# Output stage of a three-stage fp32 trunk: two inner products brought forward by a block, and another order of buffer slots

## Chip, cores, metric

The kernel runs on one core of one Trainium2 chip. The metric is the device time of one execution in microseconds. The engines are called by what they do here: TensorE (PE; PEld is its weight load), VectorE (DVE), ScalarE (ACT), GpSimd (POOL), and SP, which only issues transfers.

## The reference

One layer (DEPTH = 1), 4096 tokens of width 1024, all in float32:

```
normed = rms_norm(x, norm_w)
u, gate = split(normed @ pool_in_w)                  # 1024 -> 2 x 1024
pooled  = trailing_mean(u, window 2/4/8/16 by group) - u
mixed   = pooled @ group_w (4 groups of 256) + group_b
y       = mixed * pool_scale * silu(gate)
out     = rms_norm(x + y @ pool_out_w, final_norm_w)
```

## The kernel before

**Stages.** The group map is folded into the input weights at the start. The steps in the list `steps` follow: kind "a" and kind "b" make the two halves of the channels of y for four blocks of 1024 tokens each; kind "o" is the output stage, y @ out_w with residual and final norm, for eight blocks of 512 tokens (blocks 0 to 7). The change lies in the output stage alone.

**A block of the output stage.** The matrix product of a block is done in the Strassen-Winograd way: each operand is cut into four quarters (11, 12, 21, 22), and seven products P1 to P7 of sums of quarters replace eight. They run in the order P1, P7, P6, P2, P5, P4, P3 (ORDER_OUT); each is one step. Of y, "11" and "12" make the rows of half 0, "21" and "22" those of half 1. All partial results stay in PSUM: of the eight banks a block uses four pairs, "x" (P1, P2), "v" (P7, P4), "y" (P6, P5, P3) and "spare", which rotate by three pairs from block to block. P1 is copied from x to y, so that later products add to it.

**Precision.** An operand is split into a high part (a ScalarE copy to fp32r) and a low part (a VectorE subtraction); a product is high x high, high x low and low x high. `split` issues both, `high` and `low` one each. `mm3` (L805) issues the three matmuls of a plain product, 128x512; a plain product of the output stage is 24 of them (two row quarters j, four k, three parts).

**Inner products.** P2 and P7 of a block may themselves be done by seven smaller products, the leaves: `leaf` (L947), six matmuls of 128x256 each, 42 for a product. Their weights are sums of quarters of P2's or P7's weights: `load_inner` loads the raw ones, `sum_inner` makes the sums (four VectorE subtractions or additions), `split_weight` the high and low parts, into places that are kept from the pool for good (`gathered`, six in all). Leaves P6 and P5 of inner P2 are run in the step of the outer P5, by `product_out` and `evict_o`, and `add_inner` (VectorE) adds the leaves' results to the rows. In the kernel before, inner P2 runs from block 2 on and inner P7 (`own_first`, `own_into`, `own_move`, `own_add`) from block 3 on: OWN = 3. The table `forming` says in which step the weights are made.

**The order.** Up to P5 of block OWN - 1 a scheduler places the instructions of each engine, held by hints (`issue_after`). From P4 of block OWN - 1 on, `steady` writes the order by hand, and `InOrder` keeps each of VectorE, ScalarE, GpSimd and SP in that order; P2 of the last block turns that off again.

**Buffers.** Operands, rows and temporaries share two pools of slots, st (11) and vt (8); `take` gives the slot that has been free longest, `give` puts one at the end. So the order of `give` and `take` decides which earlier user a new one must wait for. A block's rows (x, to which the product is added) take four slots: two for half 1 (`load_h(b, 1)`), two for half 0 (`load_h(b, 0)`); each slot holds a row quarter's 1024 columns. In all blocks but the last, ScalarE writes the product into a half of the columns, x is added by an accumulating transfer that GpSimd issues (`add_h`), or loaded by SP first. `norm_row` scales the finished rows and stores them (`out<-...`, issued by GpSimd): half 1 of block b - 1 in P1's step of block b, half 0 in P6's step. In `steady`, `load_y` fetches the next block's quarters of y from DRAM (yd): 11 and 21 in P7's step, 12 and 22 in P4's step, where 11 is also split for the next P1.

Of the kernel before, what the change touches and what calls it, by code (L numbers as in the profile page):

```python
# [25 lines left out]
HIST = 16  # L26
NS = 11
NV = 8
OWN = 3
EPS = 1e-6  # L30

P1, P2, P3, P4, P5, P6, P7 = range(1, 8)
# [54 lines left out]
def kernel(  # L87
# [57 lines left out]
    st = Slots(sts)  # L145
# [826 lines left out]
    def own_add():  # L972
        bank = own["v"][1].rearrange("p (j b) -> p j b", j=2)
        add(bank, bank, own["m5"].unsqueeze(1).to_broadcast([P, 2, 256]))
# [214 lines left out]

    def split_o(b, i):  # L1190
        s = oxs[b]
        if i == P2 and b > 1:
            return split_inner(s["12"])
        t = next_op("p (s a b) -> p s a b", s=2, a=4)
        if i == P7:
            s["3"] = take("p (a b) -> p a b", a=4)
            sub(s["3"], s["11"], s["21"])
        elif i == P6:
            add(s["21"], s["21"], s["22"])
            sub(s["11"], s["21"], s["11"])  # L1200
        elif i == P3:
            sub(s["12"], s["12"], s["11"])
            give(s.pop("11"))
        key = {P1: "11", P7: "3", P6: "11", P2: "12", P5: "21", P4: "22", P3: "12"}[i]
        split(t, s[key])
        if i not in (P1, P6, P2):
            give(s.pop(key))
        return t
# [293 lines left out]
    def steady(n):  # L1502

        _, b, i = steps[n]
        sets, s, c = sets_of("o", b), oxs[b], b + 1
        final, t = c == NBO, None
        ahead = oxs[c] if not final else None
        whole = dict(a=4, s=2)
        if b < OWN:
            ready[i] = split_up.pop(n)  # L1510
        if i == P1:
            past = sets_of("o", b - 1)
            if final:
                load_h(b, 1)
            t = ready.pop(P1)
            out_part(P1, t, sets["x"][0], 0, range(4))
            square_rows(b - 1, 0, past, 0)
            copy(sets["y"][0], sets["x"][0])
            factor(b - 1, 1)
            add(s["21"], s["21"], s["22"])  # L1520
            sub(s["11"], s["21"], s["11"])
            ready[P6] = next_op("p (s a b) -> p s a b", **whole)
            split(ready[P6], s["11"])
            with tc.issue_after(latest[0]):
                out_part(P1, t, sets["x"][1], 1, range(2))
            own_first(ready.pop(P7), sets)
            with tc.issue_after(latest[0]):
                out_part(P1, t, sets["x"][1], 1, range(2, 4))
            copy(sets["y"][1], sets["x"][1])
            square_rows(b - 1, 0, past, 1)  # L1530
            for j in range(2):
                norm_row(b - 1, 1, j)
        elif i == P7:
            if final:
                load_h(b, 0)
            else:
                ahead["11"] = load_y(c, 0, 0)
                ahead["21"] = load_y(c, 1, 0)
            own_into(P2, 0)
            own_into(P6, 1)  # L1540
            own_move(2, 1)
            a11, a21, a12, a22 = row_quarters(s["12"])
            v = temp(0, "p (n k c) -> p n k c", n=4, k=2)
            sub(v[:, 0], a11, a21)
            sub(v[:, 1], a22, v[:, 0])
            add(v[:, 2], v[:, 1], a11)
            sub(v[:, 3], a12, v[:, 1])
            plain_op, both = op_halves()
            split(both, s["12"])
            root(b - 1, 0)  # L1550
            with tc.issue_after(latest[0]):
                out_part(P6, ready[P6], sets["y"][0], 0, range(2))
            own_into(P7, 2)
            own_into(P3, 1)
            own_move(3, 2)
            with tc.issue_after(latest[0]):
                out_part(P6, ready[P6], sets["y"][0], 0, range(2, 4))
            own_into(P4, 2)
            factor(b - 1, 0)
            ready[P2] = {  # L1560
                p: [plain_op[:, k, g, j] for k in range(2)]
                for p, (g, j) in {P1: (0, 0), P2: (1, 0), P4: (1, 1)}.items()
            }
        elif i == P6:
            v = temp(0, "p (n k c) -> p n k c", n=4, k=2)
            sums_op = next_op("p (s n k c) -> p s n k c", s=2, n=4, k=2)
            high(sums_op, v)
            low(sums_op, v)
            own_add()
            norm_row(b - 1, 0, 0)  # L1570
            norm_row(b - 1, 0, 1)
            for m, p in enumerate((P7, P6, P5, P3)):
                ready[P2][p] = [sums_op[:, k, m] for k in range(2)]
            ready[P5] = next_op("p (s a b) -> p s a b", **whole)
            split(ready[P5], s["21"])
            give(s.pop("21"))
            if not final:
                load_h(b, 1)
            evict_o(b, P7, sets)
            with tc.issue_after(latest[0]):  # L1580
                out_part(P6, ready.pop(P6), sets["y"][1], 1, range(4))
            evict_o(b, P6, sets)
        elif i == P2:
            if not final:
                load_h(b, 0)
            ready[P4] = next_op("p (s a b) -> p s a b", **whole)
            split(ready[P4], s["22"])
            give(s.pop("22"))
            InOrder.on = not final
            product_out(P2, ready.pop(P2), sets, False)  # L1590
            evict_o(b, P2, sets)
        elif i == P5:
            sub(s["12"], s["12"], s["11"])
            give(s.pop("11"))
            ready[P3] = next_op("p (s a b) -> p s a b", **whole)
            split(ready[P3], s["12"])
            give(s.pop("12"))
            product_out(P5, ready.pop(P5), sets, False)
            evict_o(b, P5, sets)
        elif i == P4:  # L1600
            if not final:
                ahead["12"] = load_y(c, 0, 1)
                ahead["22"] = load_y(c, 1, 1)
                ready[P1] = next_op("p (s a b) -> p s a b", **whole)
                split(ready[P1], ahead["11"])
                u = temp(0, "p (a b) -> p a b", a=4)
                sub(u, ahead["11"], ahead["21"])
                ready["own"] = op_halves()
                high(ready["own"][1], u)
            product_out(P4, ready.pop(P4), sets, False)  # L1610
            evict_o(b, P4, sets)
        else:
            if not final:
                u = temp(0, "p (a b) -> p a b", a=4)
                v = temp(1, "p (n k c) -> p n k c", n=4, k=2)
                b11, b12, b21, b22 = row_quarters(u)
                square_rows(b, 1, sets, 0)
                sub(v[:, 0], b12, b11)
                sub(v[:, 1], b22, v[:, 0])
                sub(v[:, 2], b22, b12)  # L1620
                sub(v[:, 3], b21, v[:, 1])
                sums_op = next_op("p (s n k c) -> p s n k c", s=2, n=4, k=2)
                high(sums_op, v)
                square_rows(b, 1, sets, 1)
                root(b, 1)
                plain_op, both = ready.pop("own")
                low(both, u)
                low(sums_op, v)
                ready[P7] = {
                    p: [plain_op[:, k, g, j] for k in range(2)]  # L1630
                    for p, (g, j) in {P1: (0, 0), P2: (1, 0), P3: (1, 1)}.items()
                }
                for m, p in enumerate((P5, P6, P7, P4)):
                    ready[P7][p] = [sums_op[:, k, m] for k in range(2)]
            product_out(P3, ready.pop(P3), sets, final)
            evict_o(b, P3, sets)
# [200 lines left out]
    def row_plan(b):  # L1837
# [9 lines left out]

    scales, summed = {}, []
    forming = {
        (1, P1): lambda: load_inner(P2),  # L1850
        (1, P6): lambda: sum_inner(P2),
        (1, P5): lambda: split_weight(P2, P7, P6),
        (1, P4): lambda: (split_weight(P2, P5, P4), end_weights(P2)),
        (2, P1): lambda: load_inner(P7),
        (2, P6): lambda: sum_inner(P7),
        (2, P5): lambda: split_weight(P7, P7, P6),
        (2, P4): lambda: (split_weight(P7, P5, P3), keep_temps(P7)),
    }
    forming_seven = (P7, P6, P5, P4)

    for n in range(2, len(steps)):
# [15 lines left out]
            for j in rows.get(i, ()):  # L1877
                load_row(b + 1, j // 4, j % 4, early if b == 0 and i == P7 else None)
        if kind == "o":
            while len(gathered) < 3 * min(b, 2) and st.free and len(st.free) + len(vt.free) > 4:  # L1880
                gathered.append(st.keep())
                kept.append(gathered[-1])
            if b > 0:
                keep[0] = 0
        if kind == "o" and i == P6 and late_split:
            late_split.pop()()
# [121 lines left out]
```

## Time and profile before

| | us |
|---|---|
| median of three runs | 908.83 (908.62 to 909.54) |
| the profiled execution | 908.27 |
| its span | 906.5 |
| TensorE busy | 897.4 |
| first to last matmul of the output stage | 612.81 to 899.47 |

The page gives, for each engine, its busy time and share of the span; the chain of work that ended last, followed back from the end; and the costliest groups of instructions. A row of the timeline reads: start, duration, engine, line, operation, out<-in, size, count, and in brackets how long the engine had been idle before it and what ended that. Rows with a count merge equal instructions that follow one another. VectorE, ScalarE and GpSimd instructions all stand under L79, the line of the recording helper, and are told apart by what they read and write: `op` are operands for TensorE, `bank` PSUM, `st` and `vt` the slots, `ors` and `otmp` the norm's factors.

### The profile page before, as it was taken

To read this page: it belongs to the slowest core of one execution; us is meant where nothing else is said; L and a number is where in the kernel's file an instruction comes from. 1 tells how busy PE (TensorE), PEld (TensorE's weight loads), DVE (VectorE), ACT (ScalarE), POOL (GpSimd) and SP (SyncE) were. 2 spreads that over 40 slices of the span, in tenths; PEclk is the share of its full clock that TensorE was granted. 3 is DMA by queue.
4 is the path that set the end of the run, shared out by engine and by line. 5 is a ranking of instruction groups with operands and counts; after the bars stand their busy time and mean duration, and the time that the engine had idled before them with its cause. 6 is when DMAs were issued, how large, how long until landed. Compare 5 with 4: busy or idle time off the path is not lost.

```text
span 906.5 us, 12128 instructions
## 1 busy us (share of the span) xinstructions
PE 897.4 (99%) x4482; PEld 791.3 (87%) x4482; DVE 750.8 (83%) x908; ACT 514.7 (57%) x847; POOL 116.3 (13%) x208
## 2 busy tenths in 40 slices
PE   9999999999999999999999999999999999999996
PEld 7888888888888888889889888888888898999886
DVE  3899995985995999798599499599778888888897
ACT  7869547447446465346545636654545556566554
POOL 0020100100110000000000000001223233343330
PEclk9999999999999999999999999999999999999999
DMA  9987767577575453323554474638574755846842
GB/s 339 401 307 227 273 238 241 186 269 247 224 265 199 164 193 109 101 110 116 200 195 146 179 267 152 197 123 239 174 208 142 184 162 164 232 129 167 241 161 95
DMA packets 71692, 180.49 MB, mean 199 GB/s; under 512 B 6608, under 2 KB 24656, under 8 KB 71632
## 3 DMA queue, kind: packets, MB, share of 16 engines
q1 hardware_dynamic: 54976, 132.50, 42.5%
q0 software_dynamic: 15936, 46.16, 17.1%
q10 hardware_dynamic: 720, 1.06, 0.3%
q8 instruction: 35, 0.57, 0.3%
q14 instruction: 25, 0.20, 0.1%
HBM read 118.86 MB, written 60.83 MB: 198 GB/s over the span
## 4 chain that ended last, share of the span: by engine, by line
PE 93%; DVE 2%; DMA 2%; ACT 1%; issue 1%; POOL 0%; SPq 0%; DVEq 0%; POOLq 0%; ACTq 0%
PE bank L805 84%; PE bank L947 4%; PE bank L447 3%; PE bank L751 2%; DVE vt L79 1%; DMA vt<-in_x 1%; DMA early<-in_wut 1%; DVE op L79 0%; DMA out<-vt 0%; ACT op L79 0%; DVE st L79 0%; POOL otmp L79 0%; ACT vt L79 0%; PE bank L513 0%; ACT bank L79 0%
## 5 line engine op out<-in xcount | busy, mean ns | idle before, releaser
L805 PE MATMUL bank<-op,w 128*128 128x512 f32 x2592 | 560.8, 379 | 0.0
L805 PEld LDWEIGHTS bank<-op,w 128*128 128x128 f32 x2592 | 489.5, 189 | 70.0 <-ACT bank L79 0.4
L805 PE MATMUL bank<-w,op 128*128 128x512 f32 (+1 forms) x1092 | 240.0, 377 | 0.5 <-DVE st L79 0.4
L805 PEld LDWEIGHTS bank<-w,op 128*128 128x128 f32 x1092 | 201.8, 189 | 27.6 <-DVE st L79 0.8
L79 DVE TENSOR_TENSOR op<-st,op 128x1024 fp32r<-128x1024 f32 x127 | 153.7, 1219 | 52.6 <-ACT op L79 52.3
L79 ACT ACTIVATE op<-st 128x1024 fp32r<-128x1024 f32 x127 | 132.9, 1050 | 64.9 <-PE bank L805 32.3
L79 ACT ACTIVATE vt<-bank 128x512 f32<-128x512 f32 (+1 forms) x136 | 76.6, 583 | 65.3 <-PE bank L805 52.7
L79 POOL DMA_DIRECT2D vt<-in_x x39 | 34.8, 985 | 398.6 <-DVE vt L79 359.8
L79 ACT ACTIVATE op<-vt 128x1024 fp32r<-128x1024 f32 x54 | 56.7, 1054 | 49.7 <-DVE vt L79 32.2
L79 DVE TENSOR_TENSOR st<-st,st 128x1024 f32<-128x1024 f32 (+1 forms) x59 | 69.7, 1199 | 17.3 <-ACT st L79 16.8
L79 DVE TENSOR_TENSOR op<-vt,op 128x1024 fp32r<-128x1024 f32 x54 | 65.8, 1220 | 16.3 <-ACT op L79 15.9
L79 DVE TENSOR_TENSOR vt<-bank,vt 128x512 f32<-128x512 f32 (+1 forms) x117 | 66.2, 594 | 12.7 <-PE bank L805 5.5
L79 ACT ACTIVATE bank<-bank 128x512 f32<-128x512 f32 (+1 forms) x75 | 37.6, 503 | 43.2 <-PE bank L805 31.6
L79 ACT ACTIVATE st<-st 128x1024 f32<-128x1024 f32 x33 | 34.8, 1056 | 23.0 <-DVE st L79 19.4
L79 DVE TENSOR_TENSOR st<-st,vt 128x1024 f32<-128x1024 f32 (+1 forms) x35 | 40.3, 1169 | 2.1 <-DMA vt<-rd 2.1
L79 ACT ACTIVATE st<-bank 128x512 f32<-128x512 f32 (+1 forms) x45 | 25.7, 586 | 28.3 <-PE bank L805 17.4
L79 DVE TENSOR_TENSOR_SCAN vt<-vt,window 128x1040 f32<-128x1040 f32 x16 | 37.9, 2375 | 1.1 <-DMA yd<-vt 1.1
L79 DVE TENSOR_TENSOR w<-st,w 128x1024 fp32r<-128x1024 f32 (+1 forms) x26 | 30.8, 1197 | 9.2 <-ACT w L79 9.2
L79 DVE TENSOR_TENSOR vt<-vt 128x1024 f32<-128x1024 f32 (+3 forms) x41 | 37.6, 919 | 0.2
L79 ACT ACTIVATE w<-st 128x1024 fp32r<-128x1024 f32 (+1 forms) x26 | 26.6, 1035 | 18.2 <-PE bank L805 10.7
L947 PEld LDWEIGHTS bank<-w,op 128*128 128x128 f32 x264 | 34.0, 191 | 2.3 <-DVE vt L79 1.0
L947 PE MATMUL bank<-w,op 128*128 128x256 f32 x264 | 35.0, 276 | 0.3 <-DVE vt L79 0.3
(115 smaller groups left out, 686.6 us busy)
## 6 DMA issues: line engine op xcount, KB each, us to landing
st<-in_xt SPq DMA_DIRECT2D x28, 512.0 KB, 6.3
sd<-st POOLq DMA_DIRECT2D x28, 512.0 KB, 4.5
st<-sd SPq DMA_DIRECT2D x26, 512.0 KB, 4.7
out<-vt POOLq DMA_DIRECT2D x26, 512.0 KB, 3.3
st<-yd SPq DMA_DIRECT2D x24, 512.0 KB, 8.5
st<-in_x SPq DMA_DIRECT2D x21, 512.0 KB, 6.3
vt<-in_x POOLq DMA_DIRECT2D x39, 256.0 KB, 6.8
yd<-st SPq DMA_DIRECT2D x19, 512.0 KB, 2.9
```

What stands on the lines that cost most here:

```text
L79: r = f(*args, **kwargs)
L447: latest[0] = nc.tensor.matmul(ps, a[:, kk, 2 * j + t, :], maps, start=t + m == 0, stop=t == 1 and m == len(pairs) - 1,).ins
L751: latest[0] = nc.tensor.matmul(cell(n, c).rearrange("p (a s) -> p a s", s=2), x1, x2, start=i == P1 and k + m == 0, stop=k == 1 and m == 2 ...
L805: latest[0] = nc.tensor.matmul(ps, a, b, start=start and n == 0, stop=stop and n == 2, skip_group_check=True).ins
L947: latest[0] = nc.tensor.matmul(ps, x1, x2, start=start and k + n == 0, stop=k == 1 and n == 2, skip_group_check=True,).ins
```

## The change

OWN becomes 2: inner P2 runs from block 1 on, inner P7 from block 2, and the order by hand begins a block sooner. The weights are made sooner to match: those of P2 are loaded in P4 of block 0, summed in P3 of block 0 and split in P1 and P7 of block 1; those of P7 are loaded in P7 of block 1 and made in its P6, P5 and P4. The six kept places are gathered from P4 of block 0 on. In `steady`, 11 and 21 of the next block are fetched in P2's step, behind the rows of half 0, instead of P7's step; in P6's step the slot of 21 is given back ahead of the split that still reads it. In the last block, the rows of P7 are taken out of PSUM behind those of P6 instead of ahead of them.

```diff
-OWN = 3
+OWN = 2
...
-        if i == P2 and b > 1:
+        if i == P2 and b >= OWN - 1:
             return split_inner(s["12"])
...
         elif i == P7:
             if final:
                 load_h(b, 0)
-            else:
-                ahead["11"] = load_y(c, 0, 0)
-                ahead["21"] = load_y(c, 1, 0)
             own_into(P2, 0)
...
             own_add()
+            u = s.pop("21")
+            give(u)
             norm_row(b - 1, 0, 0)
             norm_row(b - 1, 0, 1)
...
             ready[P5] = next_op("p (s a b) -> p s a b", **whole)
-            split(ready[P5], s["21"])
-            give(s.pop("21"))
+            split(ready[P5], u)
             if not final:
                 load_h(b, 1)
-            evict_o(b, P7, sets)
+                evict_o(b, P7, sets)
             with tc.issue_after(latest[0]):
                 out_part(P6, ready.pop(P6), sets["y"][1], 1, range(4))
             evict_o(b, P6, sets)
+            if final:
+                evict_o(b, P7, sets)
         elif i == P2:
             if not final:
                 load_h(b, 0)
+                ahead["11"] = load_y(c, 0, 0)
+                ahead["21"] = load_y(c, 1, 0)
...
     forming = {
-        (1, P1): lambda: load_inner(P2),
-        (1, P6): lambda: sum_inner(P2),
-        (1, P5): lambda: split_weight(P2, P7, P6),
-        (1, P4): lambda: (split_weight(P2, P5, P4), end_weights(P2)),
-        (2, P1): lambda: load_inner(P7),
-        (2, P6): lambda: sum_inner(P7),
-        (2, P5): lambda: split_weight(P7, P7, P6),
-        (2, P4): lambda: (split_weight(P7, P5, P3), keep_temps(P7)),
+        (0, P4): lambda: load_inner(P2),
+        (0, P3): lambda: sum_inner(P2),
+        (1, P1): lambda: split_weight(P2, P7, P6),
+        (1, P7): lambda: (split_weight(P2, P5, P4), end_weights(P2), load_inner(P7)),
+        (1, P6): lambda: sum_inner(P7),
+        (1, P5): lambda: split_weight(P7, P7, P6),
+        (1, P4): lambda: (split_weight(P7, P5, P3), keep_temps(P7)),
     }
...
-            while len(gathered) < 3 * min(b, 2) and st.free and len(st.free) + len(vt.free) > 4:
+            while len(gathered) < (6 if b else 3 * (i in (P4, P3))) and st.free and len(st.free) + len(vt.free) > 4:
                 gathered.append(st.keep())
                 kept.append(gathered[-1])
-            if b > 0:
+            if b > 0 or i in (P4, P3):
                 keep[0] = 0
```

## The prediction

> **What bounds the kernel now.** I read the page first, then the busy times by block of the output stage, then the matmuls in order of time.
>
> ```profile
> PE 897.4 (99%) x4482; PEld 791.3 (87%) x4482; DVE 750.8 (83%) x908; ACT 514.7 (57%) x847; POOL 116.3 (13%) x208
> PE 93%; DVE 2%; DMA 2%; ACT 1%; issue 1%; POOL 0%; SPq 0%; DVEq 0%; POOLq 0%; ACTq 0%
> ```
>
> TensorE is busy for 99% of the span and carries 93% of the chain that ended last. So only two things move the time: fewer TensorE cycles, and TensorE waits that appear or go. The windows are blocks 1, 4 and 7 of the output stage (columns: span, then busy time of PE, PEld, DVE, ACT, POOL):
>
> ```profile
> 649.10:685.40 36.30, 36.30 (x170) 31.79 (x169) 27.17 (x32) 19.78 (x38) 11.84 (x23) 1.00 0.62 174
> 756.70:792.00 35.30, 35.30 (x205) 32.04 (x205) 29.40 (x40) 20.70 (x39) 12.80 (x22) 1.00 0.63 177
> 863.20:899.40 36.20, 35.73 (x216) 32.20 (x214) 33.98 (x65) 18.97 (x42) 8.21 (x15) 1.00 0.29 107
> ```
>
> A block without an inner product takes 36.30 us, one with two takes 35.30. VectorE (DVE) is busy for 27 to 29 us of a middle block and for 34 of 36.2 in the last. It is the only engine near enough to become a bound.
>
> **Two more inner products.** Block 1 gets inner P2, block 2 gets inner P7. The rate of each form is read from start to start, since a modelled end hides the overlap:
>
> ```profile
> 612.81 88.22 PE L805 MATMUL bank<-w,op 128*128 128x512 f32 x408
> 700.87 0.83 PE L947 MATMUL bank<-w,op 128*128 128x256 f32 x6
> ...
> 702.20 1.50 PE L947 MATMUL bank<-w,op 128*128 128x256 f32 x12
> 703.54 0.83 PE L947 MATMUL bank<-inner,op 128*128 128x256 f32 x6
> ```
>
> 408 wide matmuls run from 612.81 to 700.87: 0.2158 us each. 12 narrow ones run from 702.20 to 703.54: 0.1117 each. A plain product is 24 wide ones, 5.18 us; an inner one is 7 leaves of 6 narrow ones, 4.69. Each saves 0.49, both **0.98 us**. [...]
>
> **The waits that TensorE has now.** In blocks 6 and 7:
>
> ```profile
> 848.07 0.89 PE L947 MATMUL bank<-inner,op 128*128 128x256 f32 x6
> 848.79 2.75 PE L805 MATMUL bank<-w,op 128*128 128x512 f32 x12
> 851.83 0.94 PE L947 MATMUL bank<-w,op 128*128 128x256 f32 x6 [0.29 <-DVE vt L79]
> 852.60 14.41 PE L805 MATMUL bank<-w,op 128*128 128x512 f32 x66
> ...
> 880.69 0.83 PE L947 MATMUL bank<-inner,op 128*128 128x256 f32 x6
> 881.56 0.67 PE L805 MATMUL bank<-w,op 128*128 128x512 f32 x2
> 882.66 3.72 PE L805 MATMUL bank<-w,op 128*128 128x512 f32 x16 [0.43 <-DVE st L79]
> 886.22 0.83 PE L947 MATMUL bank<-inner,op 128*128 128x256 f32 x6
> ```
>
> Against the two rates, block 6 loses 0.05 ahead of 848.79, 0.45 ahead of 851.83 and 0.10 behind it: 0.60 us. Block 7 loses 0.20 ahead of 881.56, 0.67 ahead of 882.66 and 0.11 ahead of 886.22: 0.98.
>
> Block 6: the leaf at 851.83 waits for a VectorE add that stands behind a ScalarE eviction, and that eviction waits for a place to write to (rows of ScalarE and of GpSimd, in order of time):
>
> ```profile
> 846.91 0.60 ACT L79 ACTIVATE vt<-bank 128x512 f32<-128x512 f32 x1 [3.03 <-DMA out<-vt]
> 836.45 1.24 POOL L79 DMA_DIRECT2D out<-vt x2 [0.42 <-DVE vt L79]
> 842.57 0.61 POOL L79 DMA_DIRECT2D out<-vt  x1 [2.10 <-DVE vt L79]
> ```
>
> The store issued at 842.57 frees the place only at 846.91, 4.3 us later. Giving a slot back ahead of its last reader in P6's step issues nothing; it turns the order of slots, so that the first halves of block b get the places of the half stored at 836.45, six us sooner; by the same 4.3 us these are free near 841, well ahead of the eviction. The wait goes, and VectorE comes to that add with some 3 us to spare: **0.60 us** saved. What is late next there is the next block's input, taken up as the second rival.
>
> Block 7: the edit takes P6's rows out of PSUM ahead of P7's, so P5 may start 1.2 us (two adds) sooner. But the queue on VectorE there has no gap to give (in order of time):
>
> ```profile
> 877.20 2.48 DVE L79 SCALAR_TENSOR_TENSOR vt<-vt,ors,st 128x1024 f32<-128x1024 f32 x2
> 879.60 1.22 DVE L79 TENSOR_TENSOR op<-st,op 128x1024 fp32r<-128x1024 f32 x1
> 880.73 2.47 DVE L79 TENSOR_TENSOR st<-bank,st 128x512 f32<-128x512 f32 x4
> 883.12 1.21 DVE L79 TENSOR_TENSOR op<-st,op 128x1024 fp32r<-128x1024 f32 x1
> 884.26 1.61 DVE L79 TENSOR_TENSOR vt<-bank,vt 128x512 f32<-128x512 f32 x3
> ```
>
> P5 can follow the first of the four adds (done at 881.4) instead of the third. Its 18 matmuls then run to 885.3, where the leaf P6 stands. That leaf may not write before the third add of the last row has read its bank; by the order of the changed kernel this add has the same work ahead of it as now and ends at 884.26 + 1.61 = 885.9. So the leaf starts 0.3 us sooner than 886.22, not 0.98, and what follows on VectorE is the same string of work to the end: **0.30 us** saved. Moving P7's rows back costs nothing: their banks are wanted by P4, which comes behind all of P5.
>
> **The transition in blocks 0 and 1.** The weights of inner P2 are now summed in block 0 (four subtractions) and split in block 1; those of P7, formerly block 2's, are all made in block 1. Block 1 thereby has four weight splits more than now, and for its inner P2 four narrow sums, one operand split and five narrow adds. The four subtractions in block 0 fall in gaps (the block is behind nothing that TensorE waits for until its banks come round again, 15 us later). The loads of these weights move from P1 of blocks 1 and 2 to P4 of block 0 and P7 of block 1 on the SP queue; one of them waits for a row's store to land, and the next block's halves queue behind it, all needed over 10 us later. I cost them at nothing; if a weight came late, the queue below would slip by as much.
>
> What counts is the VectorE queue of block 1. Its durations, from the order in time and (last row) from the groups by form:
>
> ```profile
> 657.30 1.28 DVE L79 SCALAR_TENSOR_TENSOR st<-st,ors,st 128x1024 f32<-128x1024 f32 x1 [0.92 <-POOL ors L79]
> 658.50 1.28 DVE L79 SCALAR_TENSOR_TENSOR vt<-vt,ors,st 128x1024 f32<-128x1024 f32 x1
> 659.70 1.22 DVE L79 TENSOR_TENSOR op<-st,op 128x1024 fp32r<-128x1024 f32 x1
> 660.84 0.68 DVE L79 TENSOR_TENSOR vt<-vt 128x512 f32<-128x512 f32 x1
> ...
> 663.61 1.22 DVE L79 TENSOR_TENSOR op<-vt,op 128x1024 fp32r<-128x1024 f32 x1
> L79 DVE TENSOR_TENSOR vt<-bank,vt 128x256 f32<-128x256 f32 x30 | 11.7, 419 | 5.5 <-ACT vt L79 3.1 <-PE bank L947 2.2
> ```
>
> From the norm at 657.30 to the add that frees the bank of leaf P6, the changed order has 17 instructions: two norms at 1.20 from start to start, three weight splits at 0.60 (as the four adds at 880.73), two narrow sums at 0.35 (0.42 less the overlap of neighbours), one subtraction and four operand splits at 1.14, the four sums of P7's weights (660.84 to 663.61, 2.77), and the add itself, 0.42. Together 13.8 us: the add ends at 671.1. TensorE comes to leaf P6 after 240 wide matmuls and 30 narrow from 612.81 (of the wide, 168 are block 0's, 72 block 1's), plus the 12 of P5's first half: 612.81 + 252 x 0.2158 + 30 x 0.1117 = 670.5. It waits about 0.5, and a restart costs 0.1 as at 852.60: **0.6 us lost**. The other operands of block 1 come 2 us ahead of their use by the same count. Below, this could be nothing (the norm starts 0.6 sooner); above, 1.8 (a weight or a store lands a us late).
>
> The norm's start hangs on GpSimd (rows of both engines):
>
> ```profile
> 655.15 1.22 DVE L79 TENSOR_TENSOR st<-st,st 128x1024 f32<-128x1024 f32 x1
> 655.39 1.04 POOL L79 TENSOR_TENSOR otmp<-ors,oms 128x2 f32<-128x2 f32 x1 [0.40 <-DVE ors L79]
> 656.51 0.20 POOL L79 TENSOR_TENSOR otmp<-otmp,ors 128x2 f32<-128x2 f32 x1
> ```
>
> One GpSimd step took 1.04 us until a VectorE subtraction was over, the next 0.20. [...]
>
> **The sum.** 908.27 for the profiled execution (span 906.5 and 1.8 around it) - 0.98 - 0.60 - 0.30 + 0.6 = 907.0. The median of the three runs is 0.56 above that execution, so 908.83 - 1.28 = **907.5 us**. A difference under 0.2% (1.8 us) is about what a measurement can't tell from no change; faster means below 907.0, slower above 910.6.
>
> **Rival 1, faster:** block 1's queue is in time and block 7 gives all. For it: 0.6 us is the end of a sum of 17, and each of its waits could fall out. Against: the last block's VectorE rows have no gap. Time: 908.83 - 0.98 - 0.60 = 907.2 at least, with 0.3 to 0.98 from block 7: 906.3 to 906.9. **0.32.**
>
> **Rival 2, slower:** the next block's first two halves used to be loaded in P7's step for the block after; now in P2's step, and wanted in P4's step of the same block. The second waits for a store to land (846.91 in block 6) and for what is ahead of it on SP. The transfers issued from 770 to 790 us (the last column is us to landing), and rows around block 6's end:
>
> ```profile
> st<-yd SPq DMA_DIRECT2D x3, 512.0 KB, 12.6
> vt<-yd SPq DMA_DIRECT2D x1, 512.0 KB, 14.0
> 855.80 1.22 DVE L79 TENSOR_TENSOR vt<-vt,st 128x1024 f32<-128x1024 f32 x1
> 860.05 2.50 DVE L79 TENSOR_TENSOR op<-vt,op 128x1024 fp32r<-128x1024 f32 x2
> 866.85 1.50 PE L947 MATMUL bank<-w,op 128*128 128x256 f32 x12
> ```
>
> In block 4 such loads took 12.6 and 14.0 us. From 846.9 that is 859.5 to 860.9; the subtraction (855.80) to the last split (862.55) takes 6.75, so the operand stands at 866.3 to 867.7, and the leaf wants it at 866.85. A landing over 13.2 us stalls TensorE, by up to 0.85 + 0.1 in each of blocks 2 to 6: 907.5 + 4.8 = 912.3. Against: those loads stood in one heap with the row loads; now the row loads and the first half leave 3 to 6 us sooner, and I expect some 8 us. **0.16.**
>
> **Rival 3, no gain:** the wait at 851.83 comes back at the new loads without stalling the leaf, or block 1 loses 1.8: 908.3 to 909.4. **0.10.** The forecast keeps **0.42**, of which 0.08 lies below 907.0.
>
> So faster 0.32 + 0.08 = 0.40, same 0.34 + 0.09 = 0.43, slower 0.16 + 0.01 = 0.17. The range runs from rival 1's end with 0.3 of spread between runs to rival 3's: 906.0 to 909.6; rival 2 is left out.
>
> **What would show it.** Right: 84 more narrow matmuls and 48 fewer wide ones; no ScalarE wait for out<-vt; a TensorE wait of 0.3 to 1.0 on VectorE at leaf P6 of block 1; in block 7 a wait of 0.6 at the same leaf, the end 0.3 sooner. Wrong: a wait on the loads from yd ahead of the P1 or own leaves in blocks 2 to 6, or DVE with gaps in block 1.

## The result, and the profile after

| | before | after |
|---|---|---|
| median us | 908.68 (908.18 to 909.54, 6 runs) | 912.57 (911.78 to 914.26, 6 runs) |
| profiled execution (span) | 908.27 (906.5) | 912.55 (910.8) |

The changed kernel is slower by under half a percent, but clear of the noise: ratio 1.0046, interval 1.0033 to 1.0059, 3.9 us. The forecast was 907.5.

Here are, from the page of the changed kernel, the busy times and the chain of waits by engine; below them three windows (span, then busy time of PE, PEld, DVE, ACT, POOL): blocks 1, 4 and 7 of its output stage.

```profile
PE 898.1 (99%) x4518; PEld 791.4 (87%) x4518; DVE 757.7 (83%) x925; ACT 516.8 (57%) x853; POOL 120.1 (13%) x208
PE 83%; DMA 7%; DVE 5%; ACT 2%; issue 2%; POOL 0%; SPq 0%; DVEq 0%; ACTq 0%; POOLq 0%
```

```profile
650.80:687.10 36.30, 35.99 (x187) 31.80 (x186) 33.63 (x50) 22.18 (x40) 10.18 (x21) 1.00 0.70 189
757.70:793.90 36.20, 35.61 (x206) 32.03 (x205) 30.31 (x41) 21.33 (x40) 13.75 (x22) 1.00 0.65 174
865.20:901.20 36.00, 33.77 (x196) 30.00 (x195) 34.28 (x62) 19.71 (x42) 9.32 (x16) 1.00 0.33 121
```

TensorE issues 36 matmuls more, 84 narrow ones in place of 48 wide: the two inner products are there. But DMA and VectorE now carry 12% of the chain, where they carried 4%, and TensorE stands idle in block 4, in which it had no gap before. Its waits in order of time:

```profile
672.75 0.94 PE L947 MATMUL bank<-inner,op 128*128 128x256 f32 x6 [0.31 <-DVE vt L79]
...
764.99 0.94 PE L947 MATMUL bank<-w,op 128*128 128x256 f32 x6 [0.59 <-ACT bank L79]
...
872.58 0.94 PE L947 MATMUL bank<-w,op 128*128 128x256 f32 x6 [0.69 <-ACT bank L79]
...
886.03 4.12 PE L805 MATMUL bank<-w,op 128*128 128x512 f32 x18 [1.30 <-DVE st L79]
890.39 0.94 PE L947 MATMUL bank<-inner,op 128*128 128x256 f32 x6 [0.24 <-DVE vt L79]
```

Summed as excess over 0.2158 us for a wide and 0.1117 for a narrow matmul, from start to start, TensorE loses 0.58 in block 1, 1.67 in blocks 3 to 6 (before: 0.75) and 3.00 in the last (before: 0.97). In blocks 4 to 7 one place comes back each time: the second pair of own leaves (the leaves of inner P7) in P7's step (764.99), behind a ScalarE move.

Together TensorE loses 3.5 us more than before; less 0.98 for the two products, the output stage is 2.5 us longer. The two profiled spans differ by 4.3 us. The other 1.7 arise ahead of the output stage, where no instruction differs: it began at 614.54 after and at 612.81 before, and between 612.5 and 614.9 over all profiled runs here, in no order of the edits. The medians differ by 3.9; where other executions lose the rest no trace shows.

The order on ScalarE at those leaves, after and before:

```profile
763.60 1.06 ACT L79 ACTIVATE op<-vt 128x1024 fp32r<-128x1024 f32 x1 [1.09 <-DVE vt L79]
764.57 0.36 ACT L79 ACTIVATE bank<-bank 128x256 f32<-128x256 f32 x1
```

```profile
759.89 1.06 ACT L79 ACTIVATE op<-st 128x1024 fp32r<-128x1024 f32 x1
761.94 0.37 ACT L79 ACTIVATE bank<-bank 128x256 f32<-128x256 f32 x1 [0.98 <-PE bank L947]
```

VectorE's queue beside it, after and before:

```profile
761.11 2.46 DVE L79 TENSOR_TENSOR vt<-vt,vt 128x1024 f32<-128x1024 f32 x2
764.70 1.23 DVE L79 TENSOR_TENSOR op<-vt,op 128x1024 fp32r<-128x1024 f32 x1 [1.12 <-ACT op L79]
765.84 1.28 DVE L79 SCALAR_TENSOR_TENSOR st<-st,ors,st 128x1024 f32<-128x1024 f32 x1
```

```profile
757.40 2.46 DVE L79 TENSOR_TENSOR st<-st,st 128x1024 f32<-128x1024 f32 x2
762.13 2.48 DVE L79 SCALAR_TENSOR_TENSOR vt<-vt,ors,st 128x1024 f32<-128x1024 f32 x2
```

Block 4 starts at 757.7 after and 756.5 before. VectorE's add and subtraction for P6's operand start 3.4 us into the block instead of 0.9, and the first norm at 8.1 instead of 5.6: **VectorE is 2.5 us late**. Its operand goes to ScalarE's high copy (763.60), and the move of the own leaf stands behind that copy. Before, the first pair of own leaves ended at 761.90 and the move started at 761.94; after, they ended at 763.09 and the move starts only at 764.57. So TensorE waits for a move whose own input was there 1.5 us earlier.

Why VectorE is late stands in the block before. VectorE in P5's and P4's steps of block 5, after and before:

```profile
822.33 0.69 DVE L79 TENSOR_TENSOR vt<-bank,vt 128x512 f32<-128x512 f32 x1 [1.75 <-DMA vt<-in_x]
...
824.31 1.23 DVE L79 TENSOR_TENSOR vt<-st,st 128x1024 f32<-128x1024 f32 x1 [0.16 <-DMA st<-yd]
...
826.71 0.69 DVE L79 TENSOR_TENSOR vt<-bank,vt 128x512 f32<-128x512 f32 x1 [0.58 <-DMA vt<-in_x]
```

```profile
819.91 1.22 DVE L79 TENSOR_TENSOR vt<-st,vt 128x1024 f32<-128x1024 f32 x1
...
822.54 0.69 DVE L79 TENSOR_TENSOR vt<-bank,vt 128x512 f32<-128x512 f32 x1 [0.80 <-DMA vt<-in_x]
```

Three landings stand in its way, where there was one wait of 0.8 us. A block has six accumulating transfers, called row transfers from here on: two for P7's rows, two for P6's, two for half 0. VectorE waits for the second of them (822.33), for the half 21 of the next block (824.31, 0.16 us) and for the fourth (826.71). GpSimd's queue in block 5, after and before, each followed by the row of issues of its first row transfer (size, us from issue to landing):

```profile
812.17 2.75 POOL L79 DMA_DIRECT2D vt<-in_x  x3
820.00 0.86 POOL L79 DMA_DIRECT2D vt<-in_x  x1 [5.08 <-DVE st L79]
```

```profile
vt<-in_x POOLq DMA_DIRECT2D x1, 256.0 KB, 7.5
```

```profile
809.16 2.75 POOL L79 DMA_DIRECT2D vt<-in_x  x3
815.42 0.87 POOL L79 DMA_DIRECT2D vt<-in_x  x1 [3.50 <-DVE vt L79]
```

```profile
vt<-in_x POOLq DMA_DIRECT2D x1, 256.0 KB, 5.9
```

The fourth leaves 0.3 us after the first has landed (812.17 + 7.5, 809.16 + 5.9), so one late landing is passed on three transfers further. Here is SP's queue, before (the rows of half 0; then, by their order in the program, 12 and 22 of the next block and 11 and 21 of the block after it) and after (the rows; then 11, 21, 12 and 22, all of the next block). The last row is the issue of 21 after, with its time to landing:

```profile
810.39 1.88 SPq L79 DMA_DIRECT2D vt<-in_x  x2
812.33 1.53 SPq L79 DMA_DIRECT2D st<-yd  x2
813.96 1.17 SPq L79 DMA_DIRECT2D vt<-yd  x1
815.19 1.36 SPq L79 DMA_DIRECT2D st<-yd  x1
```

```profile
806.99 0.35 SPq L79 DMA_DIRECT2D vt<-in_x  x1
808.36 0.35 SPq L79 DMA_DIRECT2D st<-in_x  x1
812.35 3.83 SPq L79 DMA_DIRECT2D st<-yd  x3
816.29 0.96 SPq L79 DMA_DIRECT2D vt<-yd  x1
```

```profile
st<-yd SPq DMA_DIRECT2D x1, 512.0 KB, 10.9
```

Before, SP ran ahead of the program: 11 and 21 left a whole block before their use and could land at any time. Now 11 leaves 3.7 us sooner in the block, but both are wanted in the same block, and 11 runs beside the row transfers from the start (812.35 against 812.17; before, the first load from yd left 3.2 us after the first of these).

So far this is read off; the experiments take it apart. They use the landings in block 4, counted from its first matmul, as the measure. Ratios are to the kernel before, run beside each of them (908.3).

### The profile page after: what moved, and what is told of

Same layout as the page of the kernel before. It is cut to its first block, busy times and chain, and to the rows that moved or that the text cites. A ratio compares the mean times of both kernels' runs of the same rounds, so it can differ in the third digit from the quotient of the medians.

```text
span 910.8 us, 12218 instructions
## 1 busy us (share of the span) xinstructions
PE 898.1 (99%) x4518; PEld 791.4 (87%) x4518; DVE 757.7 (83%) x925; ACT 516.8 (57%) x853; POOL 120.1 (13%) x208
## 3 DMA queue, kind: packets, MB, share of 16 engines
q0 software_dynamic: 15936, 46.16, 17.4%
## 4 chain that ended last, share of the span: by engine, by line
PE 83%; DMA 7%; DVE 5%; ACT 2%; issue 2%; POOL 0%; SPq 0%; DVEq 0%; ACTq 0%; POOLq 0%
PE bank L805 75%; PE bank L947 5%; DVE vt L79 2%; PE bank L751 2%; DMA vt<-in_x 2%; DMA early<-in_wut 2%; DMA st<-in_x 2%; DVE st L79 1%; ACT op L79 1%; DVE op L79 1%; ACT vt L79 0%; PE bank L447 0%; DMA st<-wod 0%; DMA out<-vt 0%; SPq L79 0%
## 5 line engine op out<-in xcount | busy, mean ns | idle before, releaser
L805 PE MATMUL bank<-w,op 128*128 128x512 f32 (+1 forms) x1044 | 230.5, 377 | 1.3 <-DVE st L79 1.3
L805 PEld LDWEIGHTS bank<-w,op 128*128 128x128 f32 x1044 | 192.3, 189 | 26.4 <-issue 1.5
L79 DVE TENSOR_TENSOR op<-st,op 128x1024 fp32r<-128x1024 f32 x116 | 141.1, 1222 | 48.4 <-ACT op L79 48.0
L79 ACT ACTIVATE op<-st 128x1024 fp32r<-128x1024 f32 x116 | 121.4, 1051 | 67.0 <-PE bank L805 27.0
L79 ACT ACTIVATE op<-vt 128x1024 fp32r<-128x1024 f32 x67 | 70.6, 1057 | 73.8 <-DVE vt L79 55.6
L79 ACT ACTIVATE vt<-bank 128x512 f32<-128x512 f32 (+1 forms) x124 | 69.2, 579 | 47.7 <-PE bank L805 41.6
L79 DVE TENSOR_TENSOR op<-vt,op 128x1024 fp32r<-128x1024 f32 x67 | 81.4, 1222 | 14.0 <-ACT op L79 13.7
L79 POOL DMA_DIRECT2D vt<-in_x x26 | 23.6, 947 | 390.2 <-DVE vt L79 358.1
L79 DVE TENSOR_TENSOR vt<-bank,vt 128x512 f32<-128x512 f32 (+1 forms) x94 | 54.2, 603 | 10.1 <-DMA vt<-in_x 4.6
L79 ACT ACTIVATE st<-bank 128x512 f32<-128x512 f32 (+1 forms) x58 | 33.0, 587 | 30.2 <-PE bank L805 20.7
L79 DVE TENSOR_TENSOR st<-bank,st 128x512 f32<-128x512 f32 (+1 forms) x68 | 41.0, 624 | 8.7 <-PE bank L805 4.0
```

Of the source, the lines that this page charges most:

```text
L79: r = f(*args, **kwargs)
L805: latest[0] = nc.tensor.matmul(ps, a, b, start=start and n == 0, stop=stop and n == 2, skip_group_check=True).ins
```

## Experiments, first set: the parts

**Products alone** (`inner_only`):

```diff
-OWN = 3
+OWN = 2
 ... (and the earlier weights; loads, slots, eviction order as before)
```

> The kernel before with OWN = 2 and the earlier weights of the inner products alone; the loads, the slots and the eviction order of the last block stay as before. Theory A (the new order of loads and slots makes VectorE late in blocks 2 to 6 and in the last, which costs some 4 us): two products save 0.98, block 1 loses 0.6, so 908.3 us, between 907.7 and 909.0, and the TensorE waits of 0.76, 0.44 and 0.85 us at leaves in the blocks from 764 us on are not there. Theory B (the inner products themselves, with the order by hand begun a block sooner, make VectorE late for good): 911.5 to 912.5, with those waits.

909.19 us, ratio 1.0003 (0.9995 to 1.0012). No wait in blocks 3 to 6; block 1 loses 0.58; but the last block loses 2.58:

```profile
882.96 0.67 PE L805 MATMUL bank<-w,op 128*128 128x512 f32 x2 [1.30 <-DVE st L79]
884.07 3.72 PE L805 MATMUL bank<-w,op 128*128 128x512 f32 x16 [0.43 <-DVE st L79]
```

In block 6 the fourth row transfer had landed 32.3 us into the block, beside 1 MB of row loads for the last block, and VectorE came into block 7 2.0 us late. Theory A had expected 909.0 at most and was short by that; B is out. One thing more: block 6 loses nothing here, though loads and slots are as before and ScalarE still waits there for out<-vt (1.98 us at 843.54). So the 0.60 us that the prediction credited to the early return of a slot comes with the earlier products alone.

**Loads and slots alone** (`slots_only`):

```diff
-            else:
-                ahead["11"] = load_y(c, 0, 0)
-                ahead["21"] = load_y(c, 1, 0)
...
+            u = s.pop("21")
+            give(u)
...
-            split(ready[P5], s["21"])
-            give(s.pop("21"))
+            split(ready[P5], u)
...
                 load_h(b, 0)
+                ahead["11"] = load_y(c, 0, 0)
+                ahead["21"] = load_y(c, 1, 0)
```

> The kernel before with the next block's 11 and 21 fetched in P2's step and the slot of 21 given back ahead of its last reader, and nothing else; OWN = 3. Theory A: slower, 908.7 plus 2.5 to 4 us, so 911.2 to 912.7, with TensorE waits at the leaves of blocks 3 to 6 and the ScalarE wait for out<-vt gone. Theory B: 908.1 (the old wait of 0.60 us in block 6 goes, nothing comes).

912.24, ratio 1.0040 (1.0026 to 1.0055): the whole loss, with OWN = 3. Theory A holds: the new loads and slots are the cause.

**Eviction order of the last block alone** (`evict_only`):

```diff
             if not final:
                 load_h(b, 1)
-            evict_o(b, P7, sets)
+                evict_o(b, P7, sets)
             ... (product and eviction of P6)
+            if final:
+                evict_o(b, P7, sets)
```

> The kernel before with the rows of P7 taken out of PSUM behind those of P6 in the last block, and nothing else. The prediction's step: 0.3 us faster, 908.4, P5 starting 0.9 sooner and the leaf P6 behind it waiting 0.6. If instead P5's wait does not hang on the order of these adds: 908.7, the wait of 0.67 us unchanged.

907.89, ratio 0.9995 (0.9986 to 1.0004), which by itself can't be told from no change. The trace can: TensorE loses 0.77 in the last block instead of 0.97. P5 starts 0.2 late and then runs without a break, and the leaf P6 behind it loses 0.5, near the 0.6 expected.

```profile
882.33 4.12 PE L805 MATMUL bank<-w,op 128*128 128x512 f32 x18
886.70 0.94 PE L947 MATMUL bank<-inner,op 128*128 128x256 f32 x6 [0.24 <-DVE vt L79]
```

**Loads back in P7's step** (`loads_back`) and **slot given back late again** (`give_back`), each undone alone in the changed kernel:

```diff
+            else:
+                ahead["11"] = load_y(c, 0, 0)
+                ahead["21"] = load_y(c, 1, 0)
...
                 load_h(b, 0)
-                ahead["11"] = load_y(c, 0, 0)
-                ahead["21"] = load_y(c, 1, 0)
```

> The changed kernel with 11 and 21 of the next block fetched in P7's step again; inner products, slot given back early and eviction order as changed. Theory A, if the place of the loads is what costs: 907.5 to 908.5. Theory A, if the early return of the slot is what costs (first halves in other slots): 911 to 912.5. Theory B: 911.5 to 913.

```diff
-            u = s.pop("21")
-            give(u)
...
-            split(ready[P5], u)
+            split(ready[P5], s["21"])
+            give(s.pop("21"))
```

> The changed kernel with the slot of 21 given back behind its last reader again, as before; the loads in P2's step, the inner products and the eviction order stay as changed. Theory C (queue of additions): the early return is what lets SP issue the row loads 5 us and the loads from yd 1.5 us sooner, into the time in which GpSimd's first accumulating transfers run; without it these loads wait for the stores again, the fourth accumulating transfer of a middle block lands near 30.5 us after the block's start, VectorE comes to the norms of half 1 at 5.6 to 6.6, and the time is 908.0 to 909.0. Theory D (the recorded rival: the halves 11 and 21 themselves are late because they leave only in P2's step): VectorE waits on yd, 911 to 913.

loads_back 913.08, ratio 1.0050 (1.0038 to 1.0062); give_back 911.78, ratio 1.0034 (1.0021 to 1.0046). Neither half alone cures it. With `inner_evict` below (908.62) the square is full: with the products and the eviction order in place, the early return alone adds 4.5 us (loads_back), the moved loads alone 3.2 (give_back), both 4.0 (the changed kernel). What VectorE waits for among transfers from 690 to 880 us (total, times, longest), loads_back first:

```profile
DVE vt L79 <- DMA vt<-in_x: 12.0, 8, 3.2
```

```profile
DVE vt L79 <- DMA vt<-yd: 3.1, 1, 3.1
DVE vt L79 <- DMA st<-yd: 1.6, 1, 1.6
DVE st L79 <- DMA st<-in_x: 0.5, 1, 0.5
```

With the early return alone VectorE waits only for rows; with the moved loads alone nearly only for yd. Theory C, as I had it for give_back, fell: there the row loads still left early, 13.4 us into block 4, which I put down to the older slots that they take once 11 and 21 take theirs behind them. Two landings are at work; with the next two runs this became theory E: either is enough to make VectorE late.

What the early return does to the rows stands in the flight of the first row transfer, from issue to landing, in blocks 3 to 6. Where the slot is given back early and the stores stay in place (after, slots_only, loads_back, after_late12, after_no21), SP's next load leaves 0.1 to 0.2 us behind that transfer, and its flight takes 6.3 to 8.5 us, in the median 7.3. Where the slot is given back late (before, inner_only, inner_evict, evict_only, ie_rows_sums, give_back), the next load leaves 1.2 us or more behind it, and the flight takes 5.1 to 6.4, in the median 5.9. By kernel the medians are 7.1 to 7.4 against 5.8 to 6.1. The kernels differ in other things too, but all eleven fall in line.

## Experiments, second set: the two landings

**12 loaded later** (`after_late12`):

```diff
-                ahead["12"] = load_y(c, 0, 1)
+                ahead["12"] = take("p (a b) -> p a b", a=4)
 ...                                               # P3's step:
+                scalar.dma_start(out=ahead["12"], in_=yd[c][:, 4:8, TH : 2 * TH])
```

> The changed kernel with the load of the next block's 12 (512 KB) issued by ScalarE in P3's step instead of by SP in P4's, about 33 us after the block's start instead of 22.5. Theory C: with 512 KB fewer beside them the accumulating transfers land 1 to 2 us sooner, the fourth below 31.5 us after the block's start, VectorE is on time and the waits of TensorE at leaves in blocks 3 to 7 (2.6 us) go, in the last block 0.7 more: 909.0, between 908.0 and 910.0. Theory D: 21 leaves at the same place, its load is shared with less, and lands a little sooner: 910.5 to 912.

911.36, ratio 1.0030 (1.0019 to 1.0042). Taking 512 KB away moved the landings by only 0.4 (21) to 0.9 us (second row transfer): a miss for theory C, which had expected 910.0 at most.

**Row transfers first** (`after_accum`), in P6's step on GpSimd's queue:

```diff
-            norm_row(b - 1, 0, 0)
-            norm_row(b - 1, 0, 1)
+            for j in range(2):
+                scale_row(b - 1, 0, j)             # VectorE's part only
 ...
                 evict_o(b, P7, sets)
+                for j in range(2):
+                    store_row(b - 1, 0, j)         # GpSimd's store, behind add_h
```

> The changed kernel with the two stores of half 0 of the block before issued on GpSimd's queue behind the accumulating transfers of P7's rows instead of ahead of them, so that the first accumulating transfer leaves about 3 us sooner; all loads on SP stay where they are. Theory C: the fourth leaves and lands 2 to 3 us sooner, VectorE waits for no row, the leaves of blocks 3 to 6 do not wait: 908.5, between 907.7 and 909.5. Theory D: the halves from yd share the DMA engines with more accumulating traffic and land no sooner; VectorE's wait for 21 stays: 911.5 to 913.

909.40, ratio 1.0009 (1.0000 to 1.0018), inside theory C's range; but VectorE is not on time (norm at 7.8). It waits for no row, and only for yd (690 to 880 us):

```profile
DVE vt L79 <- DMA vt<-yd: 5.3, 3, 2.7
DVE vt L79 <- DMA st<-yd: 3.7, 2, 1.9
```

**21 not waited for** (`after_no21`: it forms the next P7's operand without half 21, and so leaves P7's true result out), and **both** (`after_accum_no21`, which leaves it out too):

```diff
-                sub(u, ahead["11"], ahead["21"])
+                sub(u, ahead["11"], ahead["11"])
```

> The changed kernel with one input replaced: the operand of the next P7 (in P4's step) is formed as 11 minus 11 instead of 11 minus 21, so that VectorE does not wait there for 21; the load itself stays, and P7's result is left out in effect. Theory E (two landings make VectorE late, either is enough: the half 21, and the accumulating transfers of the rows): the waits on yd (2.5 us in all) go, those on the rows' accumulating transfers stay and take their place; norms of half 1 at 7 to 8 us after a block's start, 911.0 to 912.3. Theory D (21 alone): VectorE on time, 908.3 to 909.3. Theory C (the rows alone): unchanged, 912.0 to 913.0.

> Both: the changed kernel with the stores of half 0 behind the accumulating transfers of P7's rows, and 11 minus 11 in place of 11 minus 21 (P7's result is left out in effect). Theory E: VectorE waits for neither, comes to the norms of half 1 at 5.6 us after a block's start, no leaf of blocks 3 to 7 waits, and the last block loses 0.8 us instead of 3.0: 907.3, between 906.7 and 908.2. Theory C or D alone: as one of the two single runs, 909.4 or above.

after_no21 912.26, ratio 1.0044 (1.0030 to 1.0058), with more waiting for rows (4.6 and 2.6 us in the changed kernel):

```profile
DVE vt L79 <- DMA vt<-in_x: 8.2, 7, 2.3
DVE st L79 <- DMA st<-in_x: 5.2, 3, 2.7
```

Both: **907.54**, ratio 0.9986 (0.9977 to 0.9994). No wait of VectorE on a transfer is left in blocks 3 to 6, TensorE loses nothing there, and the norm starts 5.6 us into blocks 3 to 6. By the medians, taking away the rows' lateness alone brings 3.2 us, 21's alone 0.3, both 5.0. The rows are the greater part, yet 21 alone still holds up VectorE. D falls by the two single runs. Their times would have fitted C as well; C falls by the run with both, for which it had 909.4 or more. That is theory E. after_accum also returns the stored rows' slots later, so its gain is that of two edits.

**Stores late, slots as before** (`ie_accum`; the diff of after_accum, on the kernel `inner_evict` below):

> A candidate: the kernel before with the inner products brought forward and the eviction order of the last block, loads and slots as before, and the two stores of half 0 behind the accumulating transfers of P7's rows. Theory C: 0.98 less for the products, 0.57 more in block 1, the 0.6 of block 6 gone, 0.3 to 0.5 less in the last block: 906.9, between 906.2 and 907.8. Theory D has no say on it (its loads are those of before); if the accumulating transfers are not what holds VectorE, the last block's 1.5 us wait of the run with the products alone stays: 908.0 to 909.

916.01, ratio 1.0090 (1.0077 to 1.0103): a miss. Here the later return of the stored rows' slots makes a ScalarE eviction wait for a store, and a leaf behind it (rows of both engines):

```profile
709.83 0.60 ACT L79 ACTIVATE vt<-bank 128x512 f32<-128x512 f32 x1 [6.02 <-DMA out<-vt]
```

```profile
713.02 0.94 PE L947 MATMUL bank<-w,op 128*128 128x256 f32 x6 [3.32 <-DVE vt L79]
```

It is the wait at 851.83 of the kernel before, in five blocks: an edit to a queue that also moves a `give` is two edits. VectorE, with the fourth row transfer landed at 28.3 us, was on time here (norm at 5.6), and the last block lost 0.76.

**All but loads and slots** (`inner_evict`), and a **candidate** (`ie_rows_sums`) on top of it:

```diff
-                sync.dma_start(                    # last block, rows of half 1
+                (sync if half == 0 else scalar).dma_start(
...
-        (1, P6): lambda: sum_inner(P7),
-        (1, P5): lambda: split_weight(P7, P7, P6),
+        (1, P5): lambda: (sum_inner(P7), split_weight(P7, P7, P6)),
```

> The changed kernel without its new order of loads and slots: inner products and eviction order of the last block alone. Theory E: 909.19 (products alone) less 0.3 to 0.5 in the last block: 908.7, with VectorE late by 2 us only in the last block, where the fourth accumulating transfer of block 6 lands late beside the last block's row loads. If the parts simply add: 908.33 + 0.86 - 0.44 = 908.75. If the changed kernel's loss lay in the pair of products and eviction order: 911 to 912.5.

> A candidate: inner products and eviction order as in the changed kernel, loads and slots as before, and two more edits: the last block's rows of half 1 (1 MB) are loaded from ScalarE's queue at the start of the last block instead of from SP in the middle of block 6, and the sums of P7's weights stand in P5's step of block 1 instead of P6's. Theory E: the fourth accumulating transfer of block 6 lands near 31 us instead of 32.3, VectorE enters the last block on time, its P5 waits 0.2 instead of 1.5, and the leaf P6 of block 1 does not wait: 908.33 - 0.98 - 0.60 - 0.2 = 906.5, between 906.0 and 907.6. If the last block's wait has another cause: 908.0 to 908.7.

inner_evict 908.62, ratio 0.9998 (0.9990 to 1.0007): the time is as expected, but in its profile VectorE enters the last block only 0.6 late, not 2, and P5 loses 0.4 there. The candidate **906.72**, ratio 0.9984 (0.9976 to 0.9993): faster than both kernels. The leaf P6 of block 1 and P5 of the last block, in its profile:

```profile
671.85 0.83 PE L947 MATMUL bank<-inner,op 128*128 128x256 f32 x6
...
882.37 4.55 PE L805 MATMUL bank<-w,op 128*128 128x512 f32 x20 [0.23 <-DVE st L79]
```

The leaf no longer waits, and P5 only 0.23. Which of its two edits brings how much was not run apart. Its profile is that of its slowest run (908.65), and holds a wait of 0.77 at a leaf of block 2; that of after_accum is its slowest too (911.40), with a wait of 1.6 us at 222 us, where no edit reaches.

The landings in block 4 and what followed (us after the block's first matmul; "–": loaded a block earlier; in brackets: landed, but not waited for; losses of TensorE summed as above):

| kernel | median us | second row transfer | 21 | fourth row transfer | norm starts | lost in blocks 3–6, last |
|---|---|---|---|---|---|---|
| before | 908.3 to 908.7 | 26.1 | – | 30.6 | 5.6 | 0.7, 1.0 |
| inner_only | 909.19 | 24.9 | – | 30.4 | 5.7 | 0.0, 2.6 |
| inner_evict | 908.62 | 25.9 | – | 31.3 | 7.7 | 0.6, 1.0 |
| ie_rows_sums | 906.72 | 24.9 | – | 30.9 | 5.6 | 0.0, 0.5 |
| after | 912.57 | 28.4 | 30.1 | 33.1 | 8.1 | 1.7, 3.0 |
| slots_only | 912.24 | 28.4 | 30.5 | 33.0 | 8.0 | 2.6, 4.2 |
| loads_back | 913.08 | 28.5 | – | 34.3 | 8.7 | 3.5, 3.2 |
| give_back | 911.78 | 26.2 | 30.2 | 31.7 | 7.8 | 1.7, 5.1 |
| after_late12 | 911.36 | 27.6 | 29.7 | 32.3 | 7.9 | 0.9, 3.4 |
| after_accum | 909.40 | 21.5 | 30.5 | 29.7 | 7.8 | 0.6, 2.6 |
| after_no21 | 912.26 | 27.9 | (30.5) | 33.2 | 8.6 | 1.6, 4.2 |
| after_accum_no21 | 907.54 | 20.8 | (29.6) | 28.6 | 5.6 | 0.0, 1.4 |

VectorE, when on time, takes them up at 26.4, 28.1 and 30.3 (after_accum_no21). The last-block losses of give_back and slots_only hold some 1.7 us each from a lower granted clock, 0.59 and 0.53 (last section). The norm column is one block of one execution: in inner_evict VectorE was late in blocks 3 and 4 and recovered by itself, which the kernels with the new order don't.

## Why the prediction was wrong, step by step

- **Two inner products, 0.98:** 84 narrow matmuls for 48 wide ones are there, at the rates forecast. That after_accum_no21 (907.54) meets the forecast's 907.5 is luck: the forecast was 1.28 below a before of 908.83, and this run is 0.80 below one of 908.34, with 0.7 us more lost in the last block than forecast.
- **Block 1, 0.6 lost:** 0.58, at the leaf named, and gone when the sums of P7's weights moved. Right.
- **Block 7, 0.30 gained:** 0.20 in evict_only, by the steps forecast. In the changed kernel it is lost many times over, since the step held only for a VectorE that enters the block on time: where it comes 2.0 (inner_only) to 2.6 us late (after), P5 loses 1.5 or more there.
- **Block 6, 0.60 gained: this is the step that failed.** The prediction said "Giving a slot back ahead of its last reader in P6's step issues nothing" and put the early return at 0.60 us saved. The ScalarE wait for out<-vt is gone, as forecast, but inner_only and inner_evict lose nothing in block 6 without the early return. What the early return does is +4.5 us (908.62 to 913.08). It issues nothing itself, but it turns the slots on which SP waits: with it alone (loads_back) the first row load of block 2 leaves 17.5 us into the block instead of 18.6, right behind the first row transfer (17.4), which lands at 24.8 instead of 23.8 (inner_evict); with the moved loads too, the row loads of block 4 leave 5 us sooner and the first from yd 1.4. The prediction priced the wait that went and never listed the six row transfers of each block, nor when VectorE wants them. In block 4 of the kernel before, the second landed 0.2 us ahead of its add.
- **The moved loads, put at nothing in the sum,** are the second term that failed: +3.2 us alone (inner_evict to give_back).
- **Rival 2** had the right loads and sign, but not the mechanism; that its 912.3 lies near 912.57 is luck. It put the deadline of the two halves at the leaf (13.2 us after issue), and they met that: 21 took 9.9 us in block 4 and 10.9 in block 5. The earlier deadline is VectorE's, at the subtraction, 28.1 us into the block. A VectorE instruction that waits there holds up all behind it, the norms among them; the stores follow the norms, and the next block's row transfers stand behind those stores on GpSimd's queue (in block 5, stores at 810.35 and 811.60, first transfer at 812.17). So one late landing can keep itself up from block to block. That is argued from the order; after_accum, which cuts the tie, is 3.2 us faster, but inner_evict has the tie and recovered. That rival's 0.16 came from an expected landing of "some 8 us", set against a deadline 5 us too late.
- **Where TensorE feels it:** at the own leaves, through a ScalarE move behind the high copy of P6's operand. The forecast listed no such place.

## What to carry to other kernels

List, for every transfer that an edit lets start sooner or later, the first instruction in an in-order queue that reads it, and count slack to that instruction, not to the busiest engine. A slot's order in a pool is a schedule for the DMA queues: an early `give` or a `take` moved by one step lets loads leave at other times (here SP's first row load of block 4 left 13.8 us into the block instead of 18.6). When two landings are each enough to cause a delay, undoing one can show little (0.3 us in after_no21); cure both before a theory is dropped.

## What the runs showed of the hardware that was not expected

- **GpSimd's row transfers and earlier landings.** In the traces of the two kernels, from 690 us on, each row transfer left 0.31 us or more after the landing of the third before it; of the 27 with a third before them in this stretch, 9 before and 15 after left just then (0.31). The profile names a VectorE instruction as releaser (5.08 at 820.00), long done. In block 5 after, where two stores stand ahead, the third row transfer left at 813.64, 0.31 us after the landing of the store issued at 810.35. No run tells whether the chip or the built program makes it so.
- **Time to landing.** A row load of 256 KB, issued by SP, took 2.8 us (after, 806.99; the DMA engines were busy for 0.64 of that time). An accumulating transfer of the same size, issued by GpSimd, took at least 4.1 in the output stage of the two kernels (after, 678.27; 0.79), and 5.9 to 9.8 in block 4 (the first of the six 5.9 before and 7.3 after, at 0.92 and 1.01); 512 KB from yd took up to 14.8 (after, 816.29; 0.97).
- **A lower clock after a wait.** In two profiled runs the granted clock of TensorE fell from 1.00 to 0.59 and 0.53 for a stretch after a wait; columns as in the windows above, the granted clock behind the five engines, of give_back (after 2.7 us idle) and slots_only (after 1.3 and 0.4):

```profile
872.00:876.00 4.00, 3.42 (x14) 3.32 (x15) 3.71 (x4) 3.20 (x10) 1.22 (x2) 0.59 0.00 0
```

```profile
887.00:890.60 3.60, 3.60 (x11) 2.82 (x10) 3.60 (x6) 0.00 (x0) 0.00 (x0) 0.53 0.00 0
```

It cost about 1.7 us each time, an estimate from these rows: 0.41 of 4.00 us and 0.47 of 3.60. In ie_accum TensorE waited 3.3 us (ahead of 713.02), and the granted clock stayed at 1.00 before and after. So in these three traces the length of a wait alone does not tell whether the clock falls behind it.
